# The output gate of an mLSTM stored with its one added, and applied with the inverse rms in one pass per head

## The chip, the core and the metric

The kernel runs on one core of a Trainium2 chip. The metric is the time of one execution on the device in microseconds (us), lower being better; the median of several runs counts. A core has engines that run side by side, each its own instructions in order: TensorE (PE, matrix products; its weight loads are listed as PEld), VectorE (DVE), ScalarE (ACT), GpSimd (POOL) and SyncE (SP, which here only starts DMA transfers). They wait for each other by semaphores. Matrix products land in PSUM, everything else lives in SBUF, which has 128 partitions; large arrays lie in HBM (the kernel's names ending in `_d`).

## The reference, cut to what matters

One encoder layer is applied to a prompt of 2048 tokens and a sample of 256. After an RMS norm, one projection feeds eight mLSTM heads and eight attention heads; both are joined, projected, and followed by a gated feed-forward layer with a short convolution. The change touches the end of the mLSTM:

```python
h = h_f + h_b                                                    # forward and backward scan
h = h * lax.rsqrt(jnp.mean(h * h, axis=-1, keepdims=True) + EPS) # per head of 64
h = h * mh_norm_w.reshape(M_HEADS, 1, HEAD_DIM)
return (jax.nn.sigmoid(mo) * h)                                  # the output gate
```

The sigmoid is computed as half of one plus a tanh: sigmoid(x) = 0.5 (1 + tanh(x / 2)). The factor 0.5 lies in the norm's weight `mhw`.

## The kernel before

The 2304 tokens are 18 tiles of 128 (`NT`), or 9 blocks of 256 (`NB`). Phase a projects the attention's inputs and the gates of the mLSTM. Then two generators are interleaved by `run_both`: `attention`, and `mlstm`, which treats the eight heads in four pairs p = 0 to 3. Later follow the output projection (`phase_c`), which begins beside the rest of attention, and the feed-forward phases.

For a pair, `proj_steps` goes over the 9 blocks: `proj` loads the normed input (`mn`), makes key and query (`mj`, L780) and value and gate (`mv`, L790) by 48 matrix products each, copies them out on ACT, and takes the gate's Tanh on ACT (L796, one 128x128 piece for each of two tiles) into `og`, which is stored to `og_d` by a DMA that ACT starts (L798). `mj` and `mv` share one PSUM tile (`MJ = 1`). `projT` and `upd` make the chunk states `C`, and `recur` chains them (L877). For pair 3 (`LASTP`) the steps differ: `proj_kv` makes key and value only (L808, `mj` and `mjn`), and `proj_qo` makes query and gate (L808, `mv` and `mvn`) while the pair is put out; its gate stays in SBUF transposed (`ogT`).

`out_steps` puts a pair out, tile by tile, as a pipeline: `out_l` loads a row of maxima, `out_m` masks it and loads the stored gate (`ogr`), `out_a` takes exponentials on ACT, `out_b` makes scores (`mS`) and the state's part (`mI`), `out_c` the numerator (`mN`), the division (`dn`) and `hh`, the head output of 128 tokens by two heads of 64; two ACT squares with a sum and two POOL instructions give `mr`, the inverse rms of each token and head. `out_n` multiplies `hh` by it and, for pairs 0 to 2, by the gate. `out_d` transposes `hh` on PE (`mT`), scales it on the way out of PSUM into `mmx` and stores it to `mix_d`. The output steps of pair p run beside the projections of pair p + 1; those of pair 3 run beside `proj_qo`. The PSUM tiles `mS`, `mI`, `mN`, `mT`, `mu` share two slots (tag `m`, `MB = 2`), so each waits until the one two before it has been read.

Attention takes query blocks of 512 columns: `px` (L590) and DVE's maximum `mx` (L591) for the next block, `ps` (L616, L617) for the scores, two exponentials on ACT (L620, L621), a subtraction `pl` on DVE (L622) and six `pv` products (L634). `px`, `ps`, `pq` and `pr` share four PSUM banks (tag `sc`). At a block's end DVE takes four reciprocals `rs` (L651). `phase_c` adds `wo` and `cmx`, splits of weights and inputs, to DVE's work while the last pair ends.

The source does not fix the order. The program is built with a scheduler that works out a time for every instruction (`schedule_with_timeline_sim=True`), with higher priority (`MPRI`) for the mLSTM's output steps; while attention runs with `phase_c` PE's order is that of the source. So any edit can move instructions it does not name.

Of the kernel before, what the change touches and what calls it, by code (L numbers as in the profile page):

```python
# [11 lines left out]
AF = mybir.ActivationFunctionType  # L12
ALU = mybir.AluOpType
# [4 lines left out]
P = 128  # L18
# [24 lines left out]
LASTP = 3  # L43
# [49 lines left out]
def f32(ap):  # L93
    return ap.bitcast(F32)
# [641 lines left out]
def mlstm(g, tc, s1, sp, sw, sn, pj_, pm):  # L736


    nc = g.nc
# [8 lines left out]
    def weights(p):  # L748
        s = Pair()
        s.p = p  # L750
        s.hs = slice(2 * p, 2 * p + 2)
        s.w = [sw.tile([P, 2, 512], F32R, tag="w", name=f"wm{p}_{c}", bufs=WB) for c in range(NCC)] if p else g.wm0
        for c in range(NCC if p else 0):
            load_split(g, s.w[c][:, 0, :], s.w[c][:, 1, :], g.w_m[p, c], g.raw if c % RWM < 2 else sp,
                       f"rm{p}_{c}", RST, g.n1w[:, c:c + 1], bufs=2 if c % RWM < 2 else RWM - 2)
        s.kT, s.qb, s.va, s.C, s.kw = [], [], [], [], {}
        for i in range(NT):
            s.C.append(sp.tile([P, 2, 65], F32, tag="C", name=f"C{p}_{i}", bufs=NT))
        for b in range(NB):
            s.kT.append(s1.tile([P, BT], F32, tag="kT", name=f"mkT{p}_{b}", bufs=NB))  # L760
            s.qb.append(s1.tile([P, 2, 2, P], F32, tag="qb", name=f"qb{p}_{b}", bufs=NB))
            s.va.append(s1.tile([P, 2, 2, 65], F32, tag="va", name=f"va{p}_{b}", bufs=NB))
        return s

    def steps():


        for c in range(NCC):
            for o in range(2):
                for k, ah in enumerate(((0, 0), (0, 1), (1, 0))):  # L770
                    yield c, o, k, ah

    def proj(s, b):
        nm = f"{s.p}_{b}"
        nT = [sn.tile([P, 2, 2, P], F32R, tag="nT", name=f"mn{nm}_{c}", bufs=NTB) for c in range(NCC)]
        for c in range(NCC):
            nc.sync.dma_start(f32(nT[c]), g.n1_d[b, :, c])
        pj = pj_.tile([P, 2, BT], F32, tag="mj", name="mj" + nm, bufs=MJ)
        for c, o, k, (a, h) in steps():
            nc.tensor.matmul(pj[:, o], s.w[c][:, a, o * P:(o + 1) * P], nT[c][:, :, h, :],  # L780
                             start=(c + o + k == 0), stop=(c == NCC - 1 and k == 2 and o == 1))
        nc.scalar.activation(s.kT[b], pj[:, 1], AF.Copy)
        for h in range(2):
            r = slice(64 * h, 64 * h + 64)
            nc.gpsimd.memset(s.qb[b][r, :, 1 - h, :], 0.0)
            nc.scalar.activation(s.qb[b][r, :, h, :], pj[r, 0].rearrange("p (n t) -> p n t", t=P), AF.Copy)  # L786
        og = s1.tile([P, 2, P], F32, tag="og", name="og" + nm, bufs=1)
        pv = pj_.tile([P, 2, BT], F32, tag="mj", name="mv" + nm, bufs=MJ)
        for c, o, k, (a, h) in steps():
            nc.tensor.matmul(pv[:, o], nT[c][:, o, a, :], s.w[c][:, h, 256:512],  # L790
                             start=(c + o + k == 0), stop=(c == NCC - 1 and k == 2 and o == 1))
        for o in range(2):
            i = 2 * b + o
            nc.scalar.activation(s.va[b][:, o, :, 0:64], pv[:, o, 0:P].rearrange("p (h d) -> p h d", h=2), AF.Copy,
                                 scale=g.rc[:, i:i + 1])
            nc.scalar.activation(og[:, o], pv[:, o, P:BT], AF.Tanh, scale=g.rch[:, i:i + 1])  # L796
        nc.gpsimd.memset(s.va[b][:, :, :, 64:65], 1.0)
        nc.scalar.dma_start(g.og_d[s.p, b], og)  # L798

# [144 lines left out]

    def out_n(s, i, o):
        hh, r = o.hh, o.r
        nc.vector.tensor_tensor(hh, hh, r.unsqueeze(2).to_broadcast([P, 2, 64]), ALU.mult)
        if s.p < LASTP:
            nc.vector.scalar_tensor_tensor(hh, o.og.rearrange("p (h d) -> p h d", h=2), 1.0, hh, ALU.add, ALU.mult)

    def out_d(s, i, o):
        nm = f"{s.p}_{i}"
# [25 lines left out]
    def out_steps(s):  # L978
        os_ = {}
        s.og = {}  # L980
        for i in range(NT + DLAG):
            if s.p == LASTP and i % 2 == 0 and i < NT:
                proj_qo(s, i // 2)
            if DLAG <= i:
                with tc.high_priority(offset=MPRI):
                    out_d(s, i - DLAG, os_.pop(i - DLAG))
            for lag, f in ((3, out_c), (2, out_b), (4, out_n), (1, out_a)):
                if lag <= i < NT + lag:
                    with tc.high_priority(offset=MPRI):
                        f(s, i - lag, os_[i - lag])  # L990
            if i == 0:
                os_[i] = out_l(s, i)
            if i + 1 < NT:

                with tc.issue_after(os_[i - DMB + 2].power) if i >= DMB - 2 else nullcontext():
                    os_[i + 1] = out_l(s, i + 1)
            if i < NT:
                with tc.issue_after(os_[i + 1].load.ins) if i + 1 < NT else nullcontext():
                    out_m(s, i, os_[i])
            yield (2.7 if s.p < LASTP else OW3) if i < NT else 1  # L1000

    s = weights(0)
    yield from proj_steps(s)
    for p in range(4):
# [3 lines left out]
        if p < 3:  # L1008
# [9 lines left out]
            s = s2  # L1018
# [784 lines left out]
```

## Time and profile before

| what | us |
|---|---|
| median of 3 runs (3366.43 to 3368.13) | 3366.88 |
| the profiled execution, its own time | 3374.1 |
| its span, first to last instruction | 3372.4 |
| ACT busy / POOL busy | 1802.4 / 1327.6 |
| gate's Tanh, L796, 54 of 371 ns | 20.0 |
| first and last `hh` by `mr`, L947, start | 445.9 / 1435.8 |
| first and last gate pass, L949, start | 448.0 / 1235.8 |

Durations come from one profiled execution, recorded by a hardware profiler; comparisons of time come from runs without it. A group's line gives source line, engine, operation, names of what is written and read, shapes, count, then busy us, the mean ns of one, and how long the engine stood idle before these instructions and for what. A line of a timeline gives start, length, engine and instruction, and in brackets the idle time ahead of it and who ended it. Matrix products overlap, so the length of a row of them counts, not the sum of single ones.

### The profile page before, as it was taken

How to read it: one execution, taken by the hardware profiler on the slowest of the kernel's cores; microseconds unless marked ns; L12 is line 12 of the kernel's file. 1: busy time of each engine (PE TensorE's matmuls, PEld its weight loads, DVE VectorE, ACT ScalarE, POOL GpSimd, SP SyncE). 2: the span in 40 equal slices, each digit the busy share in tenths (PEclk: the TensorE clock that was granted, in tenths of full speed). 3: DMA queues.
4: the chain of work that ended last, by engine and by line, in shares of the span. 5: the costliest groups of instructions: out<-in, count | busy, mean ns of one | idle time of the engine just before them, and what ended most of it. 6: DMA issues, size and time to landing. Idle time of an engine off the chain costs nothing. (4 is left out here: it accounts for less than half of the span.)

```text
span 3372.4 us, 57131 instructions
## 1 busy us (share of the span) xinstructions
PE 3271.5 (97%) x21366; PEld 3047.6 (90%) x21366; DVE 2403.1 (71%) x3727; ACT 1802.4 (53%) x3781; POOL 1327.6 (39%) x1686
## 2 busy tenths in 40 slices
PE   8899999999999999899999999999999999999998
PEld 6788888888888888788889999999999998999998
DVE  7875687777768788876766778877877776544573
ACT  5545666667666777665552544445555555323331
POOL 8652133213333323211246457645554442851112
PEclk9999999999999999999999999999999999999999
DMA  8765343343336444433347334424322223885563
GB/s 273 229 201 150 94 126 97 105 125 98 113 108 188 130 135 128 123 99 96 103 133 263 129 102 148 127 96 176 107 93 97 100 93 102 302 274 172 164 223 107
DMA packets 300636, 483.03 MB, mean 143 GB/s; under 512 B 36597, under 2 KB 186279, under 8 KB 300359
## 3 DMA queue, kind: packets, MB, share of 16 engines
q1 hardware_dynamic: 247543, 348.34, 32.8%
q0 software_dynamic: 36256, 121.60, 10.8%
q10 hardware_dynamic: 16560, 9.44, 0.9%
q8 instruction: 168, 2.75, 0.3%
q14 instruction: 109, 0.89, 0.1%
HBM read 337.37 MB, written 141.91 MB: 142 GB/s over the span
## 5 line engine op out<-in xcount | busy, mean ns | idle before, releaser
L622 DVE TENSOR_TENSOR pl<-ps,ph 128x512 fp32r<-128x512 f32 x520 | 354.0, 685 | 202.1 <-ACT ps L621 190.3
L1226 PE MATMUL pa<-nt,wut 128*128 128x290 f32 (+1 forms) x3168 | 449.2, 298 | 8.7 <-ACT u L1244 8.6
L620 ACT ACTIVATE ph<-ps 128x512 fp32r<-128x512 f32 x520 | 310.0, 596 | 265.7 <-PE ps L617 253.1
L1226 PEld LDWEIGHTS pa<-nt,wut 128*128 128x128 f32 x3168 | 433.1, 190 | 10.9 <-ACT u L1244 10.6
L591 DVE TENSOR_REDUCE mx<-px 128x1 f32<-128x512 f32 (+1 forms) x528 | 346.5, 674 | 100.0 <-PE px L590 98.0
L1336 DVE SCALAR_TENSOR_TENSOR y<-u,cw,y 128x1152 f32<-128x1152 f32 (+1 forms) x176 | 325.3, 1848 | 39.2 <-ACT yc L1334 17.5
L634 PE MATMUL pv<-ph,v 128*128 128x512 f32 (+1 forms) x1040 | 319.4, 402 | 0.8 <-ACT ph L620 0.3
L621 ACT ACTIVATE ps<-ps 128x512 f32<-128x512 f32 x520 | 310.3, 597 | 0.0
L1555 PE MATMUL et<-tet,wet 128*128 128x384 f32 x1584 | 279.0, 336 | 0.0
L1555 PEld LDWEIGHTS et<-tet,wet 128*128 128x128 f32 x1584 | 277.1, 188 | 0.0
L1069 PEld LDWEIGHTS po<-cmx,wo 128*128 128x128 f32 x1728 | 221.6, 191 | 9.6 <-DVE cmx L1057 1.5
L1069 PE MATMUL po<-cmx,wo 128*128 128x256 f32 x1728 | 225.8, 284 | 1.5 <-DVE cmx L1057 1.3
L1555 PE MATMUL e<-te,we 128*128 128x384 f32 x1188 | 213.9, 341 | 11.0 <-ACT te L1397 7.1
L1555 PEld LDWEIGHTS e<-te,we 128*128 128x128 f32 x1188 | 211.5, 191 | 12.0 <-ACT te L1397 7.3
L616 PE MATMUL ps<-qq,kk 128*128 128x512 f32 x520 | 215.9, 417 | 6.0 <-DVE mx L591 3.8
L780 PE MATMUL mj<-mn,wm 128*128 128x256 f32 x1296 | 200.8, 289 | 9.7 <-DMA mn<-n_d 3.9
L780 PEld LDWEIGHTS mj<-mn,wm 128*128 128x128 f32 x1296 | 185.5, 194 | 26.6 <-issue 6.8
L617 PE MATMUL ps<-qm,kl 65*128 65x512 f32 x520 | 207.6, 401 | 0.0
L590 PE MATMUL px<-kk,qq 128*128 128x512 f32 (+1 forms) x528 | 203.2, 415 | 3.9 <-DVE mx L591 2.6
L790 PEld LDWEIGHTS mv<-wm,mn 128*128 128x128 f32 x1296 | 181.9, 190 | 17.8 <-ACT qb L786 2.3
L790 PE MATMUL mv<-wm,mn 128*128 128x256 f32 x1296 | 194.8, 285 | 0.9 <-ACT qb L786 0.8
L634 PE MATMUL pv<-pl,v 128*128 128x512 f32 x520 | 192.2, 401 | 0.0
(307 smaller groups left out, 7216.9 us busy)
## 6 DMA issues: line engine op xcount, KB each, us to landing
mn<-n_d SPq DMA_DIRECT2D x216, 256.0 KB, 3.4
ru<-w_up SPq DMA_DIRECT2D x88, 512.0 KB, 3.6
a_d<-y POOLq DMA_DIRECT2D x88, 288.0 KB, 2.6
a_d<-tc POOLq DMA_DIRECT2D x66, 288.0 KB, 2.8
n_d<-n1T SPq DMA_DIRECT2D x18, 1024.0 KB, 5.7
dm<-nm_d POOLq DMA_DIRECT2D x72, 256.0 KB, 4.0
mjn<-n_d SPq DMA_DIRECT2D x72, 256.0 KB, 3.5
mvn<-n_d SPq DMA_DIRECT2D x72, 256.0 KB, 3.1
```

Of the source, the lines that this page charges most:

```text
L591: nc.vector.tensor_reduce(s.mx[:, t, z0:z0 + 1], ps[:, 0:w], AX.X, ALU.max)
L616: nc.tensor.matmul(ps, kk[:, kc:kc + P], s.qq[:, 0:N], start=True, stop=False)
L620: nc.scalar.activation(ph, ps, AF.Exp)
L621: nc.scalar.activation(ps, ps, AF.Exp)
L622: nc.vector.tensor_tensor(pl, ps, f32(ph), ALU.subtract)
L634: nc.tensor.matmul(s.pv[0:HD if k in (1, 3) else P, 0:N], v, p, start=(kp == 0 and k == 0), stop=(2 * kp + 2 == s.nk and k == 5))
L780: nc.tensor.matmul(pj[:, o], s.w[c][:, a, o * P:(o + 1) * P], nT[c][:, :, h, :], start=(c + o + k == 0), stop=(c == NCC - 1 and k == 2 and ...
L790: nc.tensor.matmul(pv[:, o], nT[c][:, o, a, :], s.w[c][:, h, 256:512], start=(c + o + k == 0), stop=(c == NCC - 1 and k == 2 and o == 1))
L1069: nc.tensor.matmul(po[:, o], wo[z // 2][c][:, a, n], mx[c][:, h, :], start=(c == 0 and k == 0), stop=(c == NCC - 1 and k == 2))
L1226: nc.tensor.matmul(p[:, z], w[:, aa, c, :], ops[k][:, c, bb, z * m:z * m + m], start=c == 0 and i == 0 and not add, stop=c == NCC // 2 - 1 ...
L1336: nc.vector.scalar_tensor_tensor(y[:, s:e], u[:, s + k:e + k], cw[:, k, jj:jj + 1], y[:, s:e], ALU.mult, ALU.add)
L1555: nc.tensor.matmul(ps[m // 2][:, m % 2], w[:, aa, m * P:(m + 1) * P], t[:, bb], start=p == 0 and n == 0, stop=p == NP - 1 and n == 2)
```

## The change

`proj` adds one to the whole gate tile of a block (128x256, both tiles of tokens) on ACT with one instruction, before it is stored. `out_n` then has no one to add: for pairs 0 to 2 it makes, for each of the two heads, one VectorE pass that multiplies 64 columns of `hh` by that head's inverse rms (a scalar for each partition) and by the gate. Before, one pass multiplied both heads by the inverse rms (128 columns), and one added one to the gate and multiplied. Pair 3 keeps its pass.

```diff
@@ proj
             nc.scalar.activation(og[:, o], pv[:, o, P:BT], AF.Tanh, scale=g.rch[:, i:i + 1])
+        nc.scalar.activation(og, og, AF.Identity, bias=1.0)
         nc.gpsimd.memset(s.va[b][:, :, :, 64:65], 1.0)
         nc.scalar.dma_start(g.og_d[s.p, b], og)
@@ out_n
         hh, r = o.hh, o.r
-        nc.vector.tensor_tensor(hh, hh, r.unsqueeze(2).to_broadcast([P, 2, 64]), ALU.mult)
-        if s.p < LASTP:
-            nc.vector.scalar_tensor_tensor(hh, o.og.rearrange("p (h d) -> p h d", h=2), 1.0, hh, ALU.add, ALU.mult)
+        if s.p == LASTP:
+            nc.vector.tensor_tensor(hh, hh, r.unsqueeze(2).to_broadcast([P, 2, 64]), ALU.mult)
+            return
+        og = o.og.rearrange("p (h d) -> p h d", h=2)
+        for h in range(2):
+            nc.vector.scalar_tensor_tensor(hh[:, h], hh[:, h], r[:, h:h + 1], og[:, h], ALU.mult, ALU.mult)
```

ACT's queue at block 5 of pair 1's projection, before and then changed (names carry numbers of their own in each program; lines behind L796 are one higher in the changed one, and four higher behind `out_n`):

```order
L794 ACTIVATE va_5_5308<-mv_5_7804,rc 128x2x64
L796 ACTIVATE og_5_7803<-mv_5_7804,rch 128x128
L794 ACTIVATE va_5_5308<-mv_5_7804,rc 128x2x64
L796 ACTIVATE og_5_7803<-mv_5_7804,rch 128x128
L941 ACTIVATE s_15_8435,mms_15_8574<-hh_15_8572 128x64 x2
L620 ACTIVATE ph_4_3_1_7082<-ps_4_3_1_7079 128x512
L621 ACTIVATE ps_4_3_1_7079<-ps_4_3_1_7079 128x512
L868 ACTIVATE C_11_5284<-mu_10_8721 64x65
L869 ACTIVATE C_11_5284<-mu_10_8721 64x65
L798 DMA og_d<-og_5_7803 128x256
```

```order
L794 ACTIVATE va_5_5317<-mv_5_7818,rc 128x2x64
L796 ACTIVATE og_5_7817<-mv_5_7818,rch 128x128
L794 ACTIVATE va_5_5317<-mv_5_7818,rc 128x2x64
L796 ACTIVATE og_5_7817<-mv_5_7818,rch 128x128
L797 ACTIVATE og_5_7817<-og_5_7817 128x256
L869 ACTIVATE C_11_5293<-mu_10_8738 64x65
L870 ACTIVATE C_11_5293<-mu_10_8738 64x65
L799 DMA og_d<-og_5_7817 128x256
```

The new pass (L797) follows the block's last Tanh, and the store of the gate stands behind it; the squares and exponentials that stood there have moved elsewhere.

DVE's queue where tile 5 of pair 0 is put out, before and then changed:

```order
L947 TENSOR_TENSOR hh_5_6378<-hh_5_6378,mr_5_6383 128x128
L949 SCALAR_TENSOR_TENSOR hh_5_6378<-ogr_4_5575,hh_5_6378 128x128
L591 TENSOR_REDUCE mx_4_5080<-px_4_2_2_5336 128x1
L864 MEMSET C_0_5273 128x65
L591 TENSOR_REDUCE mx_4_5080<-px_4_3_2_5339 128x1
```

```order
L953 SCALAR_TENSOR_TENSOR hh_5_6389<-hh_5_6389,mr_5_6394,ogr_4_5584 128x64 x2
L622 TENSOR_TENSOR pl_4_2_0_5198<-ps_4_2_0_5194,ph_4_2_0_5197 128x512
L865 MEMSET C_0_5282 128x65
L591 TENSOR_REDUCE mx_4_5089<-px_4_0_2_5339 128x1
L878 SCALAR_TENSOR_TENSOR C_1_5283<-C_0_5282,dec,C_1_5283 128x65
```

Two passes over 128 columns became two over 64, and the attention work around them is about one step of scores earlier than it was.

PE's queue at the end of pair 3, from the last products of `mv_8` on, before and then changed:

```order
L808 MATMUL mv_8_18247<-mvn_8_7_18238,wm_7_13603 128x256 x6
L954 MATMUL mT_11_18349<-ident,hh_11_18153 128x128
L590 MATMUL px_8_0_3_17291<-kk_16_12_11413,qq_8_17193 128x512
L929 MATMUL mN_14_18354<-va_7_13677,dm_14_18055 128x65 x4
L590 MATMUL px_8_1_3_17294<-kk_16_12_11413,qq_8_17193 128x512
L590 MATMUL px_8_2_3_17297<-kk_16_12_11413,qq_8_17193 128x512
L590 MATMUL px_8_3_3_17300<-kk_16_12_11413,qq_8_17193 128x512
L911 MATMUL mS_15_18373<-qb_7_13676,mkT_7_13675 128x256
L917 MATMUL mI_15_18377<-C_15_13651,qb_7_13676 128x130 x2
L954 MATMUL mT_12_18393<-ident,hh_12_18199 128x128
L929 MATMUL mN_15_18398<-va_7_13677,dm_15_18175 128x65 x4
```

```order
L809 MATMUL mv_8_18274<-mvn_8_7_18265,wm_7_13630 128x256 x2
L930 MATMUL mN_14_18381<-va_7_13704,dm_14_18082 128x65 x4
L912 MATMUL mS_15_18400<-qb_7_13703,mkT_7_13702 128x256
L590 MATMUL px_8_2_0_17247<-kk_16_0_11402,qq_8_17220 128x512
L590 MATMUL px_8_3_0_17250<-kk_16_0_11402,qq_8_17220 128x512
L590 MATMUL px_8_0_1_17253<-kk_16_4_11413,qq_8_17220 128x512
L918 MATMUL mI_15_18404<-C_15_13678,qb_7_13703 128x130 x2
L590 MATMUL px_8_1_1_17256<-kk_16_4_11413,qq_8_17220 128x512
L958 MATMUL mT_12_18420<-ident,hh_12_18226 128x128
L590 MATMUL px_8_2_1_17300<-kk_16_4_11413,qq_8_17220 128x512
L590 MATMUL px_8_3_1_17303<-kk_16_4_11413,qq_8_17220 128x512
L590 MATMUL px_8_0_2_17306<-kk_16_8_11424,qq_8_17220 128x512
```

`px_8_t_z` is the score product of query tile t with key group z for the maxima of the next block: 16 for the block. Before, four of them are left when `mv_8` ends; now fourteen are, between the output steps of pair 3.

## The prediction

> **What bounds the kernel now.** I read the page's first part, then a table of windows, then who waits for whom, then the timeline where the windows looked bad. Shares first (busy us, share of the span, instructions):
>
> ```profile
> PE 3271.5 (97%) x21366; PEld 3047.6 (90%) x21366; DVE 2403.1 (71%) x3727; ACT 1802.4 (53%) x3781; POOL 1327.6 (39%) x1686
> ```
>
> TensorE (PE) is busy 97% of the span, VectorE (DVE) 71%, ScalarE (ACT) 53%. The edited lines run only while mLSTM pairs 0 to 2 are projected and put out. The windows there (length; busy PE, PEld, DVE, ACT, POOL; granted clock; DMA):
>
> ```profile
> 448.00:1236.00 788.00, 782.63 (x4940) 684.11 (x4940) 595.23 (x1330) 543.21 (x1486) 238.55 (x484) 1.00 0.40 120
> 1236.00:1376.00 140.00, 138.41 (x854) 119.26 (x854) 116.44 (x285) 98.63 (x259) 41.46 (x76) 1.00 0.48 135
> 1376.00:1460.00 84.00, 70.78 (x371) 57.48 (x370) 74.51 (x172) 51.74 (x130) 16.51 (x30) 0.86 0.50 150
> ```
>
> From 448 to 1236 us, where all 54 old gate passes stand, PE is idle 788 - 782.63 = 5.4 us. That is the most that a lighter DVE can give back there: the matmuls are the same in number and size. From 1376 to 1460, where the last mLSTM pair ends beside attention, PE is idle 13.2 us, DVE is busy 74.5 of 84, and the clock is 0.86. So DVE counts at this **handoff**, and hardly anywhere else in the changed stretch. PE's waits, 448 to 1236 and then 1376 to 1460 (total us, times, longest):
>
> ```profile
> PE mu L866 <- ACT va L794: 1.2, 3, 0.6
> PE mt L847 <- ACT mkT L782: 1.1, 1, 1.1
> PE mj L808 <- ACT vT L816: 0.7, 1, 0.7
> PE mu L866 <- ACT C L869: 0.7, 1, 0.7
> ```
>
> ```profile
> PE mT L954 <- DVE dn L932: 3.8, 1, 3.8
> PE ps L616 <- DVE mx L591: 3.3, 1, 3.3
> PE px L590 <- DVE mx L591: 1.8, 3, 1.4
> PE mN L929 <- DVE mmx L959: 1.7, 1, 1.7
> ```
>
> In the first list no wait names `hh`, which the changed passes write; every one is on ACT. In the second every large one is on DVE, and the last pair's code there does not change.
>
> **The change, part by part.** DVE first (groups: count, busy us, mean ns):
>
> ```profile
> L947 DVE TENSOR_TENSOR hh<-hh,mr 128x128 f32<-128x128 f32 x72 | 26.7, 371 | 25.5 <-POOL mr L105 23.9 <-ACT ps L621 0.9
> L949 DVE SCALAR_TENSOR_TENSOR hh<-ogr,hh 128x128 f32<-128x128 f32 x54 | 18.9, 350 | 0.4
> L877 DVE SCALAR_TENSOR_TENSOR C<-C,dec,C 128x65 f32<-128x65 f32 x128 | 36.5, 292 | 6.1 <-ACT C L869 4.5
> L932 DVE SCALAR_TENSOR_TENSOR dn<-s 128x4 f32<-128x4 f32 x72 | 14.2, 197 | 0.6
> ```
>
> Removed: 54 multiplications at 371 ns and 54 gate passes at 350 ns. Added: 108 passes over 128x64 with a per-partition scalar. The trace has none, but L877 is the same operation over 128x65 with such a scalar: 292 ns. So DVE sheds 54 x (371 + 350 - 2 x 292) = 54 x 137 ns = 7.4 us. Bounds: 350 ns each (no gain from half the width) leaves 54 x 21 ns = 1.1 us; 197 ns each (the 128x4 row) makes it 17.7 us. I take 7.4, by the row of nearly the same shape. On the time: **0**, since PE's backlog covers `hh` there; without that cover at most the 5.4 us above.
>
> ACT gains 27 passes over `og`, 128x256, SBUF to SBUF in place. The last pair's Tanh has that form (min/median/max ns):
>
> ```profile
> L838 ACT ACTIVATE ogT<-ogT x9: 400/411/420, 1239.0 to 1405.0; 128x256 f32<-128x256 f32 x9
> ```
>
> 27 x 0.411 = 11.1 us, on an engine busy 543 of 788 us. The projection's one PSUM tile (MJ = 1) is released by the last Tanh, ahead of the new pass, so the next `mj` does not wait for it. Behind it in ACT's queue stand state copies, the score exponentials and the store of `og`. That store moves later by 0.4 us, in places past a few copies or exponentials. Its reader is the load in `out_m` (min/median/max ns, first and last start):
>
> ```profile
> L798 ACTq DMA_DIRECT2D og_d<-og x27: 326/326/339, 226.4 to 1018.0; - x27
> L897 POOL DMA_DIRECT2D ogr<-og_d x27: 539/563/611, 272.1 to 1179.5; - x27
> ```
>
> First to first it comes 46 us later, last to last 161, so the store costs 0. I cost the pass itself at 0 too: the cover is PE's queue of projection matmuls between one score tile and the next. If it were all uncovered, plus 11.1 us. Below zero it cannot go by itself.
>
> SP's and POOL's queues carry the same loads; SP's query, activation and weight loads swap places by a few rows, the most at the switch to pair 3, where four weight loads come between the `mjn` loads. Landing takes, by the page's list of DMA issues (KB each, us):
>
> ```profile
> mjn<-n_d SPq DMA_DIRECT2D x72, 256.0 KB, 3.5
> ```
>
> A block's 48 matmuls take 6 us (row 1010.61 below), so a load that is a place or two late still lands in time: 0 to +1, taken 0.
>
> **The moved order.** The build schedules by its own timing, so the two edits shuffle PE from mid pair 0 until `mT_17`; behind that the order is the same. Two places matter. At the switch from pair 2 to 3 (start, length, [idle before it <- releaser]):
>
> ```profile
> 1009.96 0.44 PE L847 MATMUL mt<-ident,mkT 128*128 128x128 f32 x2 [1.14 <-ACT mkT L782]
> 1010.61 6.01 PE L790 MATMUL mv<-wm,mn 128*128 128x256 f32 x48 [0.21 <-ACT qb L786]
> 1017.17 0.93 PE L866 MATMUL mu<-va,kw 128*128 128x130 f32 x4 [0.55 <-ACT va L794]
> ```
>
> Attention has run dry there, so `mv_8` stands as one block with 1.9 us of waits around it. Now attention lags by most of a block, and score and value matmuls stand inside `mv_8`. I take **-1.5** of the 1.9; bounds -1.9 and 0.
>
> At the handoff (PE rows, then DVE rows):
>
> ```profile
> 1377.05 1.00 PE L929 MATMUL mN<-va,dm 128*128 128x65 f32 x8
> 1381.95 0.52 PE L808 MATMUL mv<-mvn,wm 128*128 128x256 f32 x3
> 1404.15 0.45 PE L954 MATMUL mT<-ident,hh 128*128 128x128 f32 x1 [3.78 <-DVE dn L932]
> 1406.27 1.94 PE L929 MATMUL mN<-va,dm 128*128 128x65 f32 x8 [1.67 <-DVE mmx L959]
> 1418.90 1.08 PE L634 MATMUL pv<-ph,v 128*128 128x512 f32 x4
> 1419.82 0.63 PE L634 MATMUL pv<-pl,v 128*128 128x512 f32 x2
> 1427.53 0.79 PE L616 MATMUL ps<-qq,kk 128*128 128x512 f32 x1 [3.33 <-DVE mx L591]
> ```
>
> ```profile
> 1387.32 0.42 DVE L837 TENSOR_TENSOR ogT<-mv,ogT 128x256 f32<-128x256 f32 x1
> 1422.08 3.38 DVE L651 RECIPROCAL rs<-rs 64x128 f32<-64x128 f32 x4
> 1438.26 0.68 DVE L622 TENSOR_TENSOR pl<-ps,ph 128x512 fp32r<-128x512 f32 x1
> 1438.85 0.68 DVE L591 TENSOR_REDUCE mx<-px 128x1 f32<-128x512 f32 x1
> 1440.93 0.69 DVE L622 TENSOR_TENSOR pl<-ps,ph 128x512 fp32r<-128x512 f32 x1 [0.80 <-ACT ps L621]
> ```
>
> Take two points that both programs have: the end of `mv_7` (1382.3 us before, the row at 1381.95) and the `pl` of `ps_8_6_0` (1440.93). Between them PE now has 2.5 us more: 10 score and value matmuls at 0.23 us (1418.90 to 1419.82 is four of them) are 2.3, 8 small ones about 0.9, less four mLSTM ones that moved ahead, about 0.7. With the total unchanged, `mv_7` ends 2.5 us earlier. DVE's queue from `ogT_7` (row 1387.32) to that `pl` grows from 121 to 130 rows: 4 `mx` and 2 `pl` more at 0.6 us start to start (1438.26 to 1438.85), 4 reciprocals at 0.84, less small ones: 2.4 + 1.2 + 3.4 - 0.5 = +6.5 us. If none of it finds room: 6.5 - 2.5 = **+4.0**. If it fills gaps: before, `ogT_7` came 5.0 us after `mv_7`'s end; now fewer reduces stand ahead of it, and I count about 2.7, which is 2.3 us gained; DVE also idles 9.5 us in the window. Half of that filled gives 4.0 - 2.3 - 4.7 = -3.0; all of it, -7.8. I take **-1**, between unfilled and half filled, since each output step is a chain of DVE, ACT and POOL in turn that leaves some gaps whatever the order.
>
> The clock stands in that too. After the waits of 3.78 and 3.33 us PE is slow: the eight `mN` rows take 1.94 us where they took 1.00 before.
>
> ```profile
> 1400.00:1420.00 20.00, 14.10 (x62) 11.25 (x61) 18.34 (x53) 10.29 (x28) 2.83 (x6) 0.74 0.28 76
> 1420.00:1440.00 20.00, 16.67 (x65) 12.56 (x65) 18.20 (x38) 10.76 (x27) 4.31 (x7) 0.83 0.09 23
> ```
>
> The granted clock is 0.74 and 0.83; at half rate that is about 10 and 7 us slow. Taking out the idle 5.9 and 3.3 us leaves some 8 us of work at half rate, 4 us lost. The Trainium skill, "TensorE: Matmul & The Clock Gate", section "What's actually happening", says that the clock halves after an idle window of about 3.4 us and returns after about as long a busy one. The trace agrees with the two waits. By that rule a handoff whose gaps stay short loses nothing to the clock, and the sum would be -5 instead of -1 here; this is in the second case below.
>
> **Sum**: 0 + 0 - 1.5 - 1 = -2.5 us. The profiled execution took 3374.1 us (span 3372.4 and 1.7 around it), which makes 3371.6; the runs' median, 3366.88, lies 7.2 below it, and I move it by the same: **3364.4 us**.
>
> **The cases.** A measurement of this kernel can tell about 0.2%, 6.7 us, from no change.
> - *Forecast*, same, 0.58: PE's backlog hides both edits and the handoff ends within a few us of before. For it: 5.4 us idle in 788. Against it: the handoff can move either way. 3364.4, own range 3360 to 3373.
> - *The handoff closes*, 0.25: before, the twelve `px` of the next block were spent before `mv_8` ended, and the chain then ran alone with waits of 3.78 and 3.33 us. Now fourteen of sixteen `px` stand between the chain's steps, so no wait is long, the clock stays up, and DVE's gaps are filled. -7.8 - 1.9 - 4 would be the most; -11 gives 3356. Against it: each `px` costs DVE 0.6 us and PE 0.23, so PE waits anyway.
> - *DVE takes over the handoff*, slower, 0.13: `mN_15` needs `s_15` read from `mI_15`, and in DVE's queue that read now stands behind seven `mx`, three `wo` and three `cmx` rows since `dm_15`. If the 6.5 us find no room, +4.0; if the many short gaps lower the clock over a stretch as long again as before, another +4: +8, 3375. It decides once more than 2.5 us of the extra are unhidden.
> - *The new ACT pass shows*, 0.04: the exponentials behind it release PE's score banks. It decides where PE's queue ahead of the bank is shorter than 0.41 us; 11.1 us in full, with no other change 3378.
> - That the pass count does not fall as said is excluded by the order: 108 half passes stand where 54 + 54 stood.
>
> **Range** 3354 to 3375, which leaves out part of the second case and of the last two. Faster by over 0.2% (under 3360.1): 0.25; within: 0.58; slower (over 3373.6): 0.17.
>
> **What would show it.** Right: the half passes near 290 ns, DVE's total down by some 7 us and ACT's up by 11; PE idle 448 to 1236 still about 5 us; waits around `mv_8` near 1010 gone; the `mv_7` end 2 to 5 us earlier, and the lead mostly kept at `ps_8_6_0`. Wrong: PE waits naming `og` or `hh`; a PE wait over 3 us in the handoff with a clock below 0.8 for longer than before; a new wait on `mn` or `wm` loads; a second stretch, behind 1460, that differs though its order does not.

## The result, and the profile after

| | before | changed |
|---|---|---|
| median of 19 timed runs | 3368.21 us (3361.39 to 3373.65) | 3372.35 us (3363.24 to 3377.12) |
| ratio, 95% interval | | 1.0013 [1.0007, 1.0019] |
| profiled execution, span | 3372.4 us | 3375.0 us |

Within 0.2%, as forecast, but to the other side: about 4 us slower where 2.5 us faster stood (2.7 ± 1.1 us over all the later comparisons together). The runs of one kernel spread by 12 us, so a profile alone can't show a difference of this size; what follows leans on timed comparisons, and on stretches of the trace that repeat from profile to profile. (In the lines of the changed kernel L797 is the new ScalarE pass, L953 the half passes; lines below them are shifted by 1 and 4.)

The changed kernel's busy line, then its windows (length; busy PE, PEld, DVE, ACT, POOL; granted clock; DMA), in the order of those of before with the switch of pairs added:

```profile
PE 3275.0 (97%) x21366; PEld 3050.8 (90%) x21366; DVE 2416.3 (72%) x3727; ACT 1810.9 (54%) x3808; POOL 1321.9 (39%) x1686
```

```profile
448.00:1236.00 788.00, 782.97 (x4970) 687.87 (x4968) 610.24 (x1331) 548.71 (x1506) 234.26 (x485) 1.00 0.41 122
1376.00:1460.00 84.00, 70.53 (x347) 54.04 (x346) 77.04 (x172) 51.27 (x125) 16.32 (x27) 0.87 0.44 132
1400.00:1420.00 20.00, 15.71 (x61) 12.54 (x61) 18.11 (x50) 7.29 (x22) 3.63 (x7) 0.65 0.19 60
1420.00:1440.00 20.00, 17.04 (x63) 11.50 (x63) 18.17 (x37) 11.88 (x26) 3.37 (x5) 0.91 0.08 20
1000.00:1035.00 35.00, 32.41 (x218) 29.75 (x218) 27.07 (x58) 20.11 (x47) 12.48 (x23) 0.95 0.76 233
```

The last of these stretches before:

```profile
1000.00:1035.00 35.00, 32.73 (x227) 29.35 (x225) 28.27 (x65) 19.14 (x46) 10.45 (x16) 1.00 0.62 202
```

ScalarE grew as foreseen (1802.4 to 1810.9), TensorE's idle time from 448 to 1236 stayed at 5.0 us, but **VectorE grew too**, by 13 us where 7 were to go: from 448 to 1236 alone it is busy 610.2 us in place of 595.2. Some 7 of the 13 are in these passes themselves (46.8 us, where the 54 old multiplications of pairs 0 to 2 took 20.7 and the gate passes 18.9). The group of the half passes (count, busy us, mean ns, idle before them and what ended it), and of the new ScalarE pass:

```profile
L953 DVE SCALAR_TENSOR_TENSOR hh<-hh,mr,ogr 128x64 f32<-128x64 f32 x108 | 46.8, 472 | 28.5 <-POOL mr L105 27.9 <-ACT ph L620 0.4 <-ACT mmx L961 0.2
L797 ACT ACTIVATE og<-og 128x256 f32<-128x256 f32 x27 | 11.5, 425 | 0.2
```

A half pass takes 472 ns, more than the whole pass (371 and 350) that it is half of. The timeline of one pair of them, VectorE and then GpSimd:

```profile
485.26 1.07 DVE L953 SCALAR_TENSOR_TENSOR hh<-hh,mr,ogr 128x64 f32<-128x64 f32 x2 [1.10 <-POOL mr L105]
486.26 0.68 DVE L622 TENSOR_TENSOR pl<-ps,ph 128x512 fp32r<-128x512 f32 x1
```

```profile
484.50 0.72 POOL L105 TENSOR_TENSOR mr<-mr,mhalf 128x2 f32<-128x2 f32 x1
485.20 0.61 POOL L885 DMA_DIRECT2D dm<-nm_d  x1
485.82 0.78 POOL L893 TENSOR_SCALAR_AFFINE_SELECT dm<-dm 128x256 f32<-128x256 f32 x2
```

The passes wait for GpSimd's inverse rms `mr` and so start at the moment when GpSimd goes on to issue a load and to mask `dm`. Sorted by what GpSimd did beside each of the 108 (worked out from the trace): 279 ns mean where it was idle (27 passes), 617 ns beside the masking (42), 466 ns beside the issue of a load (29). Of the ten others five stood beside a memset (279 ns) and four beside GpSimd's product `kw` (593 ns).

TensorE's waits, 448 to 1236 us (largest), and in the handoff, 1376 to 1460:

```profile
PE mu L867 <- ACT va L794: 3.8, 2, 2.6
```

```profile
PE px L590 <- DVE mx L591: 4.6, 5, 1.8
PE ps L616 <- DVE mx L591: 2.7, 1, 2.7
PE mN L930 <- DVE mmx L963: 2.6, 1, 2.6
PE mT L958 <- DVE dm L915: 1.4, 2, 1.1
```

The first list's 2.6 us are one wait, at the switch from pair 2 to 3, with a clock of 0.95 over 1000 to 1035 (it was 1.00 before). ScalarE's queue there, then TensorE's last two matmuls of the product that `va` copies and the row that waits:

```profile
1012.76 1.53 ACT L112 ACTIVATE wm<-rm,nw 128x512 fp32r<-128x512 f32 x2 [2.50 <-DMA rm<-w_m]
1014.20 0.57 ACT L642 ACTIVATE o<-pv 64x512 f32<-64x512 f32 x1
1014.79 0.59 ACT L643 ACTIVATE rs<-pv 64x512 f32<-64x512 f32 x1
1016.00 0.72 ACT L112 ACTIVATE wm<-rm,nw 128x512 fp32r<-128x512 f32 x1 [0.61 <-DMA rm<-w_m]
1016.74 0.37 ACT L794 ACTIVATE va<-mv,rc 128x128 f32<-128x128 f32 x1
1014.03 0.40 PE L790 MATMUL mv<-wm,mn 128*128 128x256 f32 x2
1017.25 1.09 PE L867 MATMUL mu<-va,kw 128*128 128x130 f32 x4 [2.59 <-ACT va L794]
```

ScalarE's queue at the same place before:

```profile
1011.63 2.88 ACT L112 ACTIVATE wm<-rm,nw 128x512 fp32r<-128x512 f32 x4 [0.66 <-PE mv L790]
1016.66 0.37 ACT L794 ACTIVATE va<-mv,rc 128x128 f32<-128x128 f32 x1 [2.15 <-PE mv L790]
```

Seven of pair 3's eight weight splits (`wm`) now stand ahead of `va_8`; before, four did. The later ones wait for loads that SP issues only at 1007 to 1012 us, and `va` starts at 1016.74 behind them, although its product ended at 1014.43.

### The profile page after: what moved, and what is told of

Same layout as the page of the kernel before. It is cut to its first block, busy times and chain, and to the rows that moved or that the text cites. A ratio compares the mean times of both kernels' runs of the same rounds, so it can differ in the third digit from the quotient of the medians.

```text
span 3375.0 us, 57141 instructions
## 1 busy us (share of the span) xinstructions
PE 3275.0 (97%) x21366; PEld 3050.8 (90%) x21366; DVE 2416.3 (72%) x3727; ACT 1810.9 (54%) x3808; POOL 1321.9 (39%) x1686
## 5 line engine op out<-in xcount | busy, mean ns | idle before, releaser
L1559 PE MATMUL e<-te,we 128*128 128x384 f32 x1188 | 213.8, 341 | 11.5 <-ACT te L1401 7.1
```

Of the source, the lines that this page charges most:

```text
L1559: nc.tensor.matmul(ps[m // 2][:, m % 2], w[:, aa, m * P:(m + 1) * P], t[:, bb], start=p == 0 and n == 0, stop=p == NP - 1 and n == 2)
```

## The experiments

Two theories at first. **Order**: the operations cost nothing in time; what moved is the order, and it pays at the switch and at the handoff. **Price**: the new pass, or VectorE's longer passes, cost the 4 us themselves. Each kernel was timed in turn with the kernel before; the ratio is to that.

**pass_only**: the ScalarE pass without the half passes.

```diff
+        nc.scalar.activation(og, og, AF.Identity, bias=0.0)
         nc.gpsimd.memset(s.va[b][:, :, :, 64:65], 1.0)
```

> The kernel before with the 27 Identity passes alone (bias 0, so the gate is stored as before, and out_n keeps its two full passes). Order theory: the passes cost nothing of themselves (27 x 0.42 = 11 us more on ScalarE under TensorE's backlog); the time moves only by what the new order does at the switch of pairs and at the handoff; at the switch four weight splits stand ahead of va_8 in ScalarE's queue, as in the kernel before, so TensorE's wait there stays near 0.5 us without a loss of clock: ratio 1.000, within 0.9990 to 1.0008. Price theory (the pass delays the store of the gate or what stands behind it): the +4 us of the change are here: ratio 1.0013.

Measured: 1.0009 [0.9999, 1.0018]. At the switch, from 1000 to 1035 us, the only wait of TensorE, and the window:

```profile
PE mu L867 <- ACT va L794: 0.6, 1, 0.6
```

```profile
1000.00:1035.00 35.00, 34.44 (x241) 31.45 (x240) 30.25 (x71) 20.87 (x49) 12.15 (x21) 1.00 0.63 209
```

The place is as the order theory has it, and the time isn't: the ratio fits the price theory better.

**halves_only**: the changed kernel without its new line.

```diff
-        nc.scalar.activation(og, og, AF.Identity, bias=1.0)
```

> The half passes alone, without the Identity pass: the gate's 1 is left out, so the gate is tanh alone. Collision theory: the half passes run at 440 to 480 ns mean as in the changed kernel, because they start where GpSimd has just made the inverse rms and goes on with its own work; VectorE is then about 10 us busier than in the kernel before, not 7 less. In time: order theory, six weight splits ahead of va_8, one fewer than in the changed kernel: a wait at the switch of 0 to 2 us, ratio 0.9995 to 1.0010. Price theory (VectorE's extra 10 us is what costs): ratio 1.0013 here and 1.000 for the passes alone.

Measured: 1.0007 [0.9998, 1.0015]; the half passes 476 ns mean. The wait for `va` is longer than in the changed kernel, with six splits ahead and no new pass at all:

```profile
PE mu L866 <- ACT va L794: 3.5, 1, 3.5
```

The order theory had 0 to 2 us for this wait; 3.5 is a miss of its size. Each half of the change alone is as slow, within these intervals, as both together. Prices would not add up like that, though intervals this wide don't exclude two halves of 0.0006 each.

**tiny_pass**: the kernel before with an instruction of next to no work, to change the order alone.

```diff
+        nc.scalar.activation(og[:, 0, 0:1], og[:, 0, 0:1], AF.Identity, bias=0.0)
         nc.gpsimd.memset(s.va[b][:, :, :, 64:65], 1.0)
```

> The kernel before with 27 ScalarE instructions of 128x1 (Identity with bias 0 on one column of the gate): some 27 x 0.2 = 5 us on ScalarE, next to no work, but the program's order is made anew. Order theory: the time can move by some us either way, ratio 0.9985 to 1.0015, and the traces show it at the switch of pairs and at the handoff; five splits and the attention's first steps stand ahead of va_8. Price theory: no work, no change, ratio 1.0000 within 0.0005.

Measured: 0.9995 [0.9986, 1.0003], which lies in the range of either theory.

**after_again**, the changed kernel itself.

> The changed kernel once more, for a second profile. Order theory: TensorE again waits 2 to 3 us for va_8 at the switch of pairs with a stretch of half clock behind it, and VectorE has no idle time in the first 25 us of the handoff; the half passes again at 440 to 480 ns mean. If the wait at the switch is gone in this profile while the ratio is still 1.0013, the switch is not the cause.

Measured: 1.0006 [0.9997, 1.0014]; wait for `va` 2.8 us, half passes 474 ns.

**gate_first**: of the changed kernel's order one piece put back. Four of the splits are queued behind the gate on ScalarE; their loads stay where they are.

```diff
+            with tc.issue_after(g.gate) if p == LASTP and c >= 4 else nullcontext():
-            load_split(g, s.w[c][:, 0, :], s.w[c][:, 1, :], g.w_m[p, c], ...
+                load_split(g, s.w[c][:, 0, :], s.w[c][:, 1, :], g.w_m[p, c], ...
...
-            nc.scalar.activation(og[:, o], pv[:, o, P:BT], AF.Tanh, ...)
+            g.gate = nc.scalar.activation(og[:, o], pv[:, o, P:BT], AF.Tanh, ...).ins
```

> The changed kernel with one piece of its order put back: the splits of the last four weights of pair 3 stand behind the gate of pair 2's last block in ScalarE's queue, as in the kernel before, not four of seven ahead of it. Switch theory: TensorE's wait for va at the switch falls from 2.6 to 2.8 us to under 1 us and the 3.41 us of half clock behind it go; what the splits then make late is the first product of pair 3, by 0 to 1 us; the time falls by 2 to 4 us against the changed kernel: ratio 1.0000 to 1.0006. If the switch is not the cause, the wait goes and the ratio stays at 1.0010 to 1.0013, as of the changed kernel.

Measured: 1.0001 [0.9992, 1.0010]. The wait and the window, 1000 to 1035 us:

```profile
PE mu L868 <- ACT va L795: 0.3, 1, 0.3
```

```profile
1000.00:1035.00 35.00, 34.68 (x239) 31.15 (x239) 29.41 (x66) 20.58 (x49) 12.08 (x23) 1.00 0.80 255
```

TensorE is idle 0.3 us in place of 2.6, at full clock. All of the change's operations are still in. By the traces TensorE's order differs from the changed kernel's in 12 of 21366 rows, 6 at the switch and 6 near 1420 us. That makes this the cleanest of the experiments: the orders of pass_only, halves_only, tiny_pass and halves_later differ from the changed kernel's in over 4000 rows each.

**late_halves**: `(4, out_n)` made `(5, out_n)` in the list of lags.

> The changed kernel with out_n one step later (lag 5 in place of 4): the half passes no longer start just when GpSimd has made the inverse rms and goes on with its own work. Collision theory: their mean falls from 474 ns toward the 280 ns that they take where GpSimd is idle, to 290 to 380 ns, their idle time on the rms (28 us) to under 5 us, and VectorE is 8 to 15 us less busy. In time: order theory, seven splits stand ahead of va as in the changed kernel, so the wait of 2.6 us at the switch stays and the ratio is 1.0005 to 1.0015 although VectorE sheds 10 us; price theory (VectorE's time is what costs): ratio 1.0000.

Measured: 1.0006 [0.9997, 1.0015], but the half passes still take 472 ns and wait 27.3 us for the rms: the build's own scheduling put them where they were. All four computing engines have the changed kernel's order in this trace, so it is that kernel timed once more, and it doesn't test the collision.

**before_2** and **after_3**: a profile more of each.

> The kernel before once more, for a second profile. Order theory: the wait at the switch again under 1 us without a stretch of half clock within 10 us of it; from the end of the attention's start to 1830 us the stage at 1780 to 1830 again 3 us shorter than in the two profiles of the changed kernel (50 against 52.6 and 52.9), if that difference belongs to the kernel and not to the run.

> The changed kernel, a third profile. The wait at the switch 2.6 to 2.8 us with 3.41 us of half clock, half passes at 474 ns, both as before. Stage 1780 to 1830: 52.5 to 53 us if its difference belongs to the kernel, near 50 us if it belongs to the run.

The waits for `va` came out at 0.6 and 1.9 us. The stretch from 1780 to 1830, of the same order in both, took 46.9 us in before_2 and 49.5 in after_3, so it moves by 3 us from run to run of one kernel. Over all four profiles of each it took 46.9 to 51.1 and 49.5 to 52.9 us: the ranges overlap, and a difference between the kernels at this place is neither shown nor excluded.

**gate_first_2** and **pass_only_2**: the same kernels again.

> The same kernel as gate_first, to make its interval narrower. Switch theory: the wait for va stays under 0.5 us without half clock there, and the ratio is again 0.9990 to 1.0006, below the 1.0010 of the changed kernel. If it comes out at 1.0010 or above, the first result was chance and the switch is not the cause.

> The same kernel as pass_only (the passes alone), whose ratio of 1.0009 with an interval from 0.9999 to 1.0018 fits both theories. Its order has four splits ahead of va and no wait at the switch. Switch theory: 1.0000 within 0.0006 over both times. Price theory of the pass: 1.0010 or more again, with no place in the trace that pays for it named so far.

Measured: 1.0003 [0.9994, 1.0013] and 1.0010 [1.0001, 1.0018], with TensorE idle 0.5 and 0.8 us from 1000 to 1035 (waits for `va` 0.3 and 0.6). The second is a miss of the switch theory.

**halves_later**: gate_first, and the half passes queued on VectorE behind its product of states for the tile two later.

```diff
-        nc.vector.tensor_tensor(o.s1, pI.rearrange(...), ..., ALU.mult)
+        o.last = nc.vector.tensor_tensor(o.s1, pI.rearrange(...), ..., ALU.mult).ins
...
-                        f(s, i - lag, os_[i - lag])
+                        with tc.issue_after(os_[i - 2].last) if f is out_n and i - 2 < NT else nullcontext():
+                            f(s, i - lag, os_[i - lag])
```

> gate_first with each block's half passes queued behind VectorE's work on the block two later (its product of states), some ten VectorE instructions later than now. Collision theory: GpSimd's work that follows the inverse rms is over by then, so the half passes fall from 472 ns mean to 280 to 350 ns, their idle time on the rms from 28 us to under 5 us, and VectorE sheds 12 us or more of busy time. In time, if VectorE's passes are hidden: the same as gate_first, 0.9990 to 1.0006. If the halves stay near 470 ns, what slows them isn't the work that GpSimd does right behind the rms.

Measured: 1.0010 [1.0001, 1.0020]. The group, and the page's busy line:

```profile
L954 DVE SCALAR_TENSOR_TENSOR hh<-hh,mr,ogr 128x64 f32<-128x64 f32 x108 | 30.5, 323 | 1.2 <-POOL mr L105 1.1
```

```profile
PE 3268.8 (97%) x21366; PEld 3046.1 (90%) x21366; DVE 2392.7 (71%) x3727; ACT 1812.3 (54%) x3808; POOL 1325.9 (39%) x1686
```

The collision is what made the passes long: moved off GpSimd's work they fall to 323 ns, and VectorE is busy 2392.7 us, 24 less than in the changed kernel's first profile, 16 of them in this group. The time did not fall with it: 1.0010 where 0.9990 to 1.0006 was expected. But the order is not gate_first's (4159 of TensorE's rows differ), and at the switch the first product of pair 3 now waits for a split, which none does in gate_first:

```profile
PE mj L810 <- ACT wm L112: 2.2, 1, 2.2
```

**split_first**: the kernel before with an order edge and nothing else.

```diff
+            if p == LASTP and c == 6:
+                tc.add_manual_dep(g.first, g.split.name, ...)
```

(`g.first` is the first copy of `va_8`, `g.split` the split of `wm_6`: the first is queued behind the second.)

> The kernel before with seven splits of pair 3's weights ordered ahead of va_8 in ScalarE's queue, as in the changed kernel; the order that comes out also brings the attention's first steps ahead of them, so TensorE has some 4 to 6 us of rows between the last product of pair 2 and the one that waits for va. Theory that the splits ahead of va alone cost: a wait of 2 to 3 us and half clock as in the changed kernel, ratio 1.0010. Theory that it costs only where TensorE has nothing between: a wait of 0 to 1.5 us, ratio 0.9995 to 1.0005.

Measured: 1.0010 [1.0001, 1.0018]. The window 1000 to 1035 us and TensorE's waits in it:

```profile
1000.00:1035.00 35.00, 29.09 (x166) 23.98 (x164) 27.94 (x56) 17.61 (x38) 8.58 (x10) 0.85 0.49 156
```

```profile
PE px L590 <- ACT qq L578: 2.6, 1, 2.6
PE pr L605 <- DVE m4r L599: 1.7, 1, 1.7
```

Neither theory had this: the attention's first steps did come ahead, and it is they that wait, for `qq`, which stands on ScalarE behind a split that waits 2.50 us for its load. No operation of the change is in this kernel, and it is as slow as the change.

**null_1** and **null_2** (the kernel before against itself), **after_4**, **tiny_pass_2**.

> The kernel before, timed against itself, with a third profile. If the comparison is fair, the ratio is 1.0000 within 0.0006; if what is compared with the kernel before always comes out slower, it is 1.0005 to 1.0010, and then 2 to 3 us of every ratio here, the change's own too, are not the kernel's. In the profile: the wait at the switch 0.6 us and full clock, as twice before.

> The same as null_1 once more, with a fourth profile: the ratio as there, and the stages outside 270 to 1461 us, in which no order differs, spread by some 3 us from run to run.

> The changed kernel, timed in the same job as the kernel before against itself, with a fourth profile. Order theory: ratio 1.0005 to 1.0014, above both of null_1 and null_2; bias theory: the same as null_1 and null_2. Wait for va at the switch 1.9 to 2.8 us with 1.7 us of lost clock, as three times before.

> The kernel with 27 instructions of next to no work, again. Order theory: it stays below the kernel before, 0.9990 to 1.0000, as its stage from 270 to 1461 us is 7 us shorter (1084.3 against 1091.2 us); if that ratio was chance it comes out at 1.0005 or more like most others.

Measured: 1.0003 [0.9993, 1.0014], 1.0004 [0.9996, 1.0013], 1.0003 [0.9993, 1.0012], 0.9993 [0.9983, 1.0002]. So a ratio of 1.0004 is no finding here, and the change's own first interval was on the high side: after_4 did not come out above the two comparisons of the kernel before with itself, as the order theory had expected. tiny_pass_2 stayed below 1, as expected. Behind 1467 us, where TensorE's order is the same, the four profiles of the kernel before took 1901.7 to 1905.3 us to the end.

All of them together. The three middle columns are from the traces, as differences to the mean of the kernel before's four profiles: the end of `mv_7` on TensorE (counted from its 1341st matmul at 257 to 262 us, ahead of all moved order), from there to VectorE's `pl` of `ps_8_6_0`, and the sum. "Switch" is what TensorE lost from 1000 to 1035 us: 35 less its busy time, plus 35 times one less the clock. The last column is the mean of all timed runs less 3368.3 us, the mean of 145 runs of the kernel before, with twice its standard error.

| kernel (profiles, timed runs) | switch | to `mv_7` | `mv_7` to `pl` | sum | time |
|---|---|---|---|---|---|
| before (4) | 2.3 | 0 | 0 (58.4) | 0 | 0 |
| before against itself (23) | | | | | +1.0 ± 1.5 |
| changed (4, 43) | 4.2 | -2.6 | +5.0 | +2.4 | +2.7 ± 1.1 |
| late_halves (1, 11) | 3.9 | -4.4 | +5.1 | +0.7 | +2.2 ± 1.9 |
| gate_first (2, 22) | 0.4 | -5.4 | +5.4 | 0.0 | 0.0 ± 1.4 |
| halves_only (1, 11) | 7.0 | -1.6 | +3.5 | +1.9 | +1.9 ± 1.4 |
| pass_only (2, 23) | 0.7 | -3.3 | +3.9 | +0.6 | +2.9 ± 1.6 |
| halves_later (1, 12) | 2.8 | -0.3 | +0.6 | +0.3 | +3.0 ± 2.3 |
| split_first (1, 11) | 11.2 | +0.4 | +0.3 | +0.7 | +3.2 ± 1.8 |
| tiny_pass (2, 24) | 1.9 | -7.8 | +2.5 | -5.3 | -2.4 ± 1.7 |

Over all comparisons the change costs 2.7 ± 1.1 us (0.08%), of which the comparison itself may be 1. The column "`mv_7` to `pl`" hardly varies for one order (58.5, 57.9, 58.7, 58.5 us before; 63.4, 63.3, 63.5, 63.3 in the changed kernel), so there the trace does resolve a few us.

## Why the prediction was wrong, step by step

**VectorE sheds 7.4 us, 0 on the time.** The size failed, even in its sign: + 13 us of busy time. 350 ns each was my upper bound; 472 came. The row that I took, L877's 292 ns, is right for a pass beside an idle GpSimd (279 here), and I did not ask what GpSimd does at the moment when these passes can start. The old row said it: L947 waited for `POOL mr`. The Trainium skill, "SBUF — State Buffer", section "Who interferes with whom", says that a VectorE instruction with two inputs in SBUF contends with a GpSimd instruction that reads SBUF. By that rule the half passes, with `hh` and the gate as inputs, were to take longer beside the masking of `dm`; the trace agrees (617 against 279 ns, and 279 beside a memset, which only writes). The effect on the time, 0, fits gate_first, whose half passes take 472 ns as in the changed kernel and which runs as the kernel before. halves_later takes 24 us off VectorE against the changed kernel and is no faster, but its order differs, so it shows this less well.

**ScalarE gains 11.1 us, 0 on the time.** Right in size (11.5), and no wait names the pass's output. gate_first has all 27 passes and runs as the kernel before. pass_only stays unexplained (below).

**The store and the loads, 0.** As a term of its own it failed: I asked whether a load that SP issues later still lands in time for the matmuls, and it does: none of TensorE's waits from 1000 to 1035 us names such a load. I did not ask what stands in ScalarE's queue behind the split that waits for it. `va` did. What it cost is in the next step.

**The switch, -1.5.** This is the first step that failed: 1.9 us came, from 2.3 lost to 4.2 (four profiles each: 2.3, 2.2, 2.2, 2.5 against 4.3, 4.5, 3.7, 4.1). The two old waits ahead of `mv_8` went, as the step says; the third, for `va`, grew from 0.55 to 2.59 us, with a stretch of lower clock behind it. gate_first shows cause and price: with the splits behind the gate 3.8 of the 4.2 go, and the time falls by 2.7 ± 1.6 us against the changed kernel. Against the kernel before the switch then gains 1.9, which was this step's bound. `mv_7` ends 2.8 us earlier than in the changed kernel, but that alone would not show it: 1114.9 and 1117.8 us behind the 1341st matmul against 1117.4, 1120.8, 1117.7 and 1120.9. A part of that spread is half clock elsewhere: after_again has a stretch of 3.41 us at 716 us, after_4 one at 1303.

**The handoff, -1.** The second that failed. Three of its parts were sized rightly: the ten score and value products more stand behind `mv_7` as counted, `ogT_7` follows `mv_7` after 2.8 us in place of 4.9 (2.3 gained forecast, 2.1 measured), and from there to `pl` the queue of 130 rows takes 60.6 us in place of 53.5: 7.05 more (6.5 forecast). That `mv_7` ends 2.6 us earlier, beside this step's 2.5, is luck. With the -1.5 of the switch 4.0 was forecast; the switch added 1.9 instead, so the rest is some 4.5, and 2.0 of it are not explained by the products that moved. The rows in the changed kernel's first profile:

```profile
1378.33 0.40 PE L809 MATMUL mv<-mvn,wm 128*128 128x256 f32 x2
1381.54 0.41 DVE L838 TENSOR_TENSOR ogT<-mv,ogT 128x256 f32<-128x256 f32 x1
1442.14 0.69 DVE L622 TENSOR_TENSOR pl<-ps,ph 128x512 fp32r<-128x512 f32 x1 [0.76 <-ACT ps L621]
```

What failed is the half of it that was to fill gaps. Between `ogT_7` and `pl` VectorE was idle 4.1 us before (mean of four) and 4.5 us now: nothing was filled. I had taken 9.5 us of gaps from the whole window, and between the two points there were only these 4.1. Unfilled, the step's own numbers give 6.5 - 2.5 - 2.3 = +1.7. Measured at `pl` is -2.6 + 5.0 = +2.4, with the switch's 1.9 in it: that leaves +0.5 for this step. In gate_first, whose switch loses 1.9 less than that of the kernel before, the sum of 0.0 leaves +1.9. So the step was 1.5 to 2.9 us off, and the switch, at 3.4, more. Of the cases `DVE takes over the handoff` came nearest: VectorE sets the pace there, but its +4.0 left out that `ogT_7` comes sooner, and its second 4 us did not come, as the clock was low no longer than before (0.87 against 0.86 over the handoff).

**Behind 1460.** Of the 2.4 us at `pl` TensorE shows 0.4 some 140 rows on, at 1467 us (0.2, 1.2, -1.3 and 1.4; the profiles of the kernel before lie within 0.3 of their mean there). gate_first stands at -1.9 there, 2.3 ahead of the changed kernel, close to the 2.7 in time. Why 2 us come back between the two rows was not looked into. Nor is every loss at the switch carried so far: split_first loses 8.9 us more there than the kernel before, and its `mv_7` ends only 0.4 later. From 1467 us to the end the changed kernel's four profiles took 1903.4 us in the mean (1899.9 to 1906.9) and those of the kernel before 1902.9: no difference shows.

**What stays open.** At 1467 us pass_only stands at -0.1 us against the kernel before, halves_later at -0.5, split_first at -1.5, gate_first at -1.9 and tiny_pass at -7.8; in time they were +2.9, +3.0, +3.2, 0.0 and -2.4. A part of these differences may be the comparison's own 1.0 ± 1.5; the rest was not found in any stretch of the traces. Of the change's own 2.7 its traces show 0.4 at that row. So what the splits ahead of `va` cost is shown by gate_first beside the changed kernel; where all of the loss against the kernel before lies isn't.

No version beat both kernels beyond doubt. The lowest was tiny_pass, computing what the kernel before computes: 0.9995 and 0.9993, both intervals reaching past 1.

## What to carry to other kernels

In this kernel, where one engine is busy 97% and the build orders the program anew, edits of few operations or none moved the time by -2.4 to +3.2 us. Look first at the few places where the busy engine's backlog runs out, time an edit of no work beside yours, and, to test one piece of the order, put back that piece alone, as gate_first does. An instruction that is moved up takes its wait with it: ask what stands behind it in its own in-order queue. Before splitting a VectorE pass, look at what released it: an instruction that starts when GpSimd has just finished a step runs beside GpSimd's next one.

## What the runs showed of the hardware

The same 128x64 pass took 279 ns with GpSimd idle and 617 ns beside its masking of 128x256 (593 beside its product `kw` of 128x256); beside GpSimd's issue of a load the 29 half passes took 466 ns mean, while of the 31 full multiplications beside that issue in the kernel before most stayed at 293 ns (335 mean). That the issue of a load slows them isn't explained here.

The clock fell after shorter waits than the prediction reckoned with. One wait of TensorE at the switch of 1.95, 2.10, 2.37, 2.59 or 2.79 us was each time followed by a single stretch of 3.41 us at half clock, one of 3.45 us by 6.83 us, and one of 2.20 us in halves_later by none. The shortest, in after_3, with the windows around it:

```profile
1015.42 1.01 PE L867 MATMUL mu<-va,kw 128*128 128x130 f32 x4 [1.95 <-ACT va L794]
```

```profile
1010.00:1014.00 4.00, 3.48 (x24) 2.93 (x22) 2.43 (x5) 2.48 (x4) 1.51 (x3) 1.00 1.04 339
1014.00:1018.00 4.00, 2.57 (x13) 2.44 (x14) 4.00 (x7) 3.68 (x12) 0.00 (x0) 0.77 1.05 358
1018.00:1022.00 4.00, 4.00 (x28) 3.94 (x28) 4.00 (x8) 0.00 (x0) 2.33 (x2) 0.81 0.84 276
```

So a wait of some 2 us cost 1.7 us more here, or nothing. Still shorter ones did: a wait of 1.21 to 1.24 us near 1300 us was followed by 3.41 us at half clock in after_4 and gate_first, and by none in after, after_again, after_3 and gate_first_2. What decides between the two isn't shown.
